# A two-layer streaming encoder in fp32: layer B's input projection computed from seven block products in place of eight

## The chip, the cores and the metric

One core of a Trainium2 chip runs the whole program. The metric is the device time of one execution in microseconds (us), the median of several runs. About 0.2% (4.5 us) is what a measurement of this kernel can tell from no change.

## The reference, cut to what matters

Two gated attention layers run over 2048 prompt frames and 64 sample frames (together 2112 tokens, width 1024). Each layer normalizes its input, projects it with one combined matrix, does banded attention, and projects back:

```python
def project(x, norm_g, w_in, q_g, k_g, n_heads, n_kv):
    h = rms_norm(x, norm_g)
    p = h @ w_in
    q, k, v, gate = jnp.split(p, [wq, wq + wkv, wq + 2 * wkv], axis=-1)
    q = rms_norm(q.reshape(*lead, n_heads, HEAD_DIM), q_g)
    k = rms_norm(k.reshape(*lead, n_kv, HEAD_DIM), k_g)
    return q, k, v, gate
# per layer: y = x + (attention(q, k, v) * silu(gate)) @ w_out
```

Layer A (first) has 16 heads on 2 key heads; layer B has 16 heads of 64 with their own keys. For layer B `w_in` is 1024 x 4096. For one pair of heads the columns of q, k, v and gate are 4 x 128 = 512.

## The kernel before, in words

Everything is computed in fp32 by splitting each operand into a high part and a low part (`h`, `l`, type fp32r, one pass of TensorE each) and adding three products: xh·wh, xh·wl, xl·wh.

**Layer B's projection.** The tokens are cut into eight units of 256 (two tiles of 128 tokens) and one sample unit of 64. The work runs over eight head pairs (`hp`, 0 to 7) and, inside a pair, over the nine units in the order 0 to 6, sample, 7. `project_b` (L513) computes one tile: eight blocks of 128 input features, three matmuls each of 512 columns (L527, L528, L529) into one PSUM bank (`pj`, two buffers). The stationary operand is a 128x128 block of x, the moving one a 128x512 block of the weights. `evacuate` (L622; the ACTIVATE at L635) copies the 512 columns to SBUF on ScalarE (ACT) with the tokens' RMS scale: 384 columns (q, k, v) and 128 (gate).

**Operands.** `load_b` (L542) gives a unit its four operands A11, A12, A21, A22: Aij is tile i (of two) and half j of the input features. In pair 0 they are loaded raw from `x1`, split by ACT (L553) and GpSimd (POOL, L554) into an `xx` buffer (seven of them, XN) and stored to `xo` in DRAM (512 KB each). From pair 1 on they are loaded from `xo` (L549). A unit's loads are issued when the unit before it starts.

**Weights.** `load_weights` (L282) prepares a pair's weights: eight raw loads of 256 KB, each scaled by the norm gain and split by ACT (L315) and VectorE (DVE, L318) into `wh` and `wl` (fifteen buffers each, WN). The first five are queued three units ahead, the rest one unit ahead.

**The order of the work.** TensorE (PE) follows the order in which the program is written: `Filler` (L761) hands out projection work in steps of three matmuls, and the attention pipeline (L1357) calls for a share of it between its own steps. Attention works two units behind the projection: per tile and head `scores` (L1244), then `values` (L1304, transposes and one copy at L1321: ACT for the unit's first tile, DVE for its second), then `outputs` (L1324). Side work (weights, splits, norms) goes into a background queue that is emptied in shares at these points. The other engines and the one DMA queue (SP) are ordered by the framework's scheduler at compile time. After layer B the output projection follows (L1441 to L1443).

Of the kernel before, what the change touches and what calls it, by code (L numbers as in the profile page):

```python
# [33 lines left out]
XB = 3  # L34
XR = 5
XN = 7
EARLY = 3
MORE = 4.7
WN = 15
# [14 lines left out]
def hybrid_encoder_kernel(  # L54
# [171 lines left out]
    og = [dr.tile([P, KC, TOK], F32, tag=n, name=n) for n in ("oga", "ogb")]  # L226
    x1 = dr.tile([P, KC, TOK], F32, tag="x1", name="x1")
    xs = dr.tile([P, 2 * KC * TOK], F32, tag="xsa", name="xsa")
    xo = dr.tile([P, 4 * NU + 1, 8 * P], F32, tag="xo", name="xo")

    class Item:
        pass
# [300 lines left out]
        res.append(ps)  # L533
        return cost

    SLOT = {n: i for i, n in enumerate(("A11", "A12", "A21", "A22"))}

    def operand(xx):
        v = xx[:, : 8 * P].rearrange("p (e k s) -> p e k s", e=2, k=4)
        return v[:, 0], v[:, 1]  # L540

    def load_b(unit, hp):  # L542
        u, T, tiles = unit
        x = Item()
        x.op, x.items = {}, []

        def cached(n, i):
            xx = t("xx", [P, 4 * OT], XN, F32R)
            held["last"] = load(xx[:, : 8 * P].bitcast(F32), xo[:, i]).ins  # L549
            return xx  # L550

        def split(xx, xh, xl, rv, i):
            nc.scalar.copy(xh, rv)  # L553
            nc.gpsimd.tensor_tensor(xl, rv, xh.bitcast(F32), op=ALU.subtract)  # L554
            store(xo[:, i], xx[:, : 8 * P].bitcast(F32))

        if T == TS:
            if hp:
                x.joint = cached("J", 4 * NU)[:, : 8 * P].rearrange("p (k s) -> p k s", k=8)
                return x  # L560
            raw = t("xraw", [P, 2 * OT], XR)[:, :512].rearrange("p (k s) -> p k s", k=8)
            held["last"] = load(raw, x1[:, :, SEQ:TOK]).ins

            def fn():
                xx = t("xx", [P, 4 * OT], XN, F32R)
                x.joint = v = xx[:, : 8 * P].rearrange("p (k s) -> p k s", k=8)
                split(xx, v[:, :, :TS], v[:, :, TS:], raw, 4 * NU)

            x.items.append(bg.put(0.52, fn))
            return x  # L570

        names = ("A11", "A12", "A21", "A22")
        raw = {}

        def raws():
            for e in range(2):
                for i in range(2):
                    r = t("xraw", [P, 2 * OT], XR)[:, :512].rearrange("p (k s) -> p k s", k=4)
                    held["last"] = load(r, x1[:, 4 * i : 4 * i + 4, u * UT + e * P : u * UT + e * P + P]).ins
                    raw["A%d%d" % (e + 1, i + 1)] = r  # L580

        def part(n, src):
            def fn():
                xx = t("xx", [P, 4 * OT], XN, F32R)
                xh, xl = operand(xx)
                split(xx, xh, xl, raw[src], 4 * u + SLOT[n])
                x.op[n] = xh, xl
            return fn

        if hp == 0:  # L590
            raws()
            x.items = [bg.put(0.52, part(n, n)) for n in names]
# [541 lines left out]
    def layer_b():  # L1134
# [4 lines left out]
        def add_unit(hp, unit):  # L1139
# [12 lines left out]

            def weights(*m):
                if hp not in st.emit:
                    (st.w[hp],), _, st.emit[hp] = load_weights(1, (w_in_b[hp], 512))
                st.emit[hp](*m)

            def take_qk(e, pr):
# [35 lines left out]
                    it.ready = e == len(tiles) - 1  # L1194
                    yield c

            filler.total += 8 * (6 if T == UT else 2) * 512 / 2400
            it.mark = filler.total
            filler.add(prefetch, weights if u == 0 else None, gen)

        for hp in range(8):
            for unit in order:
# [154 lines left out]
        def pipeline():  # L1357
# [231 lines left out]
```

## Time and profile before

| | |
|---|---|
| time, median of 3 runs | 2264.24 us (2262.56 to 2265.06) |
| time of the profiled execution | 2262.1 us |
| its span, first to last instruction | 2260.3 us |
| PE, DVE, ACT, POOL busy | 99%, 63%, 58%, 34% of the span |
| layer B's projection, eight pairs | 857.9 to 2047.9 us of the span |
| granted TensorE clock, mean | 0.997 |

A busy PE is counted from the start of a matmul to the modelled end of its drain, and successive matmuls overlap. So what one matmul costs in a stream is the distance between two starts, not its duration. Start times are in the timeline view.

### The profile page before, as it was taken

The numbers are of one execution on the slowest core, as the hardware profiler recorded it, in microseconds if no ns is written. First come the engines' busy times: TensorE is split into PE (matmuls) and PEld (weight loads), VectorE is DVE, ScalarE is ACT, GpSimd is POOL, SyncE is SP. The second block draws the span as 40 slices with busy tenths as digits, with TensorE's granted clock in tenths as the row PEclk, the third lists the DMA queues.
The fourth block names the chain that finished last, engine by engine and source line by source line (L and its number), as shares of the span: only waits on it lengthen the run. The fifth ranks groups of instructions, "written<-read, shape, count | busy, mean of one in ns | idle before, by whom it ended". The sixth has DMA issues, their size and how long they took to land. (4 is left out here: it accounts for less than half of the span.)

```text
span 2260.3 us, 41004 instructions
## 1 busy us (share of the span) xinstructions
PE 2231.6 (99%) x13981; PEld 1908.7 (84%) x13981; DVE 1423.0 (63%) x4168; ACT 1312.7 (58%) x3341; POOL 778.4 (34%) x1153
## 2 busy tenths in 40 slices
PE   8999999999999999999999999999999999999999
PEld 7887888888889998878888888888888888888999
DVE  7779988888785545675655655656556556565211
ACT  7888877777774335664555655545556555454321
POOL 5654533333254445431222222222222212223442
PEclk9999999999999999999999999999999999999999
DMA  8846446754446767554554544544545445443664
GB/s 281 298 144 214 165 139 184 224 179 146 158 121 193 215 188 268 186 182 142 150 148 138 158 139 142 151 145 142 148 140 160 138 137 154 139 125 113 201 182 135
DMA packets 236800, 379.26 MB, mean 168 GB/s; under 512 B 24288, under 2 KB 167024, under 8 KB 236560
## 3 DMA queue, kind: packets, MB, share of 16 engines
q1 hardware_dynamic: 236592, 376.65, 54.4%
q8 instruction: 110, 1.80, 0.3%
q14 instruction: 98, 0.80, 0.1%
HBM read 296.13 MB, written 82.08 MB: 167 GB/s over the span
## 5 line engine op out<-in xcount | busy, mean ns | idle before, releaser
L527 PE MATMUL pj<-wh,xx 128*128 128x512 f32 x1024 | 426.8, 417 | 0.0
L529 PE MATMUL pj<-wh,xx 128*128 128x512 f32 x1024 | 403.6, 394 | 0.0
L528 PE MATMUL pj<-wl,xx 128*128 128x512 f32 x1024 | 403.3, 394 | 0.0
L1285 ACT ACTIVATE p<-p,nm 128x640 f32<-128x640 f32 (+5 forms) x272 | 204.4, 751 | 236.9 <-DVE nm L1281 234.1
L1281 DVE CUSTOM_DVE_ANT_0 p<-sb,BT 128x640 f32<-128x640 f32 (+5 forms) x272 | 196.5, 722 | 173.3 <-PE sb L1275 169.5
L1441 PE MATMUL pj<-xx,wh 128*128 128x264 f32 x1024 | 295.0, 288 | 4.9 <-DVE res L1446 4.8
L389 POOL TENSOR_TENSOR xx<-xraw,xx 128x528 fp32r<-128x528 f32 (+1 forms) x168 | 225.1, 1362 | 202.9 <-ACT xx L388 197.4
L1442 PE MATMUL pj<-xx,wh 128*128 128x264 f32 x1024 | 292.1, 285 | 0.0
L1443 PE MATMUL pj<-xx,wl 128*128 128x264 f32 x1024 | 290.8, 284 | 0.0
L654 POOL TENSOR_TENSOR f<-f,mhalf 128x4 f32<-128x4 f32 (+1 forms) x136 | 137.4, 1011 | 428.9 <-DVE f L653 420.6
L613 PE MATMUL pj<-wh,xx 128*128 128x512 f32 (+1 forms) x624 | 245.9, 394 | 1.3 <-ACT pb L635 1.0
L614 PE MATMUL pj<-wl,xx 128*128 128x512 f32 (+1 forms) x624 | 233.0, 373 | 1.8 <-DVE wl L318 1.8
L615 PE MATMUL pj<-wh,xx 128*128 128x512 f32 (+1 forms) x624 | 234.1, 375 | 0.0
L527 PEld LDWEIGHTS pj<-wh,xx 128*128 128x128 f32 x1024 | 193.0, 188 | 44.9 <-issue 20.1
L529 PEld LDWEIGHTS pj<-wh,xx 128*128 128x128 f32 x1024 | 192.7, 188 | 44.8
L528 PEld LDWEIGHTS pj<-wl,xx 128*128 128x128 f32 x1024 | 193.7, 189 | 23.2
L1441 PEld LDWEIGHTS pj<-xx,wh 128*128 128x128 f32 x1024 | 193.6, 189 | 7.8 <-DVE res L1446 6.0
L635 ACT ACTIVATE pa<-pj,rms 128x384 f32<-128x384 f32 (+1 forms) x219 | 118.1, 539 | 136.7 <-PE pj L529 125.8
L1442 PEld LDWEIGHTS pj<-xx,wh 128*128 128x128 f32 x1024 | 193.3, 189 | 0.2
L1443 PEld LDWEIGHTS pj<-xx,wl 128*128 128x128 f32 x1024 | 193.5, 189 | 0.0
L388 ACT CAST xx<-xraw 128x528 fp32r<-128x528 f32 (+1 forms) x168 | 103.0, 628 | 133.0 <-PE pj L1443 112.9
L1040 ACT ACTIVATE p<-p,nm 128x257 f32<-128x257 f32 (+2 forms) x272 | 134.5, 497 | 73.5 <-DVE nm L1034 61.3
(228 smaller groups left out, 5222.1 us busy)
## 6 DMA issues: line engine op xcount, KB each, us to landing
xx<-xo SPq DMA_DIRECT2D x231, 512.0 KB, 3.6
xx<-xsa SPq DMA_DIRECT2D x88, 512.0 KB, 4.6
xraw<-oga SPq DMA_DIRECT2D x64, 264.0 KB, 3.5
xo<-xx SPq DMA_DIRECT2D x33, 512.0 KB, 4.4
xraw<-ogb SPq DMA_DIRECT2D x64, 264.0 KB, 3.4
xsa<-xx SPq DMA_DIRECT2D x32, 512.0 KB, 4.2
wraw<-in_w_in_b_dram SPq DMA_DIRECT2D x64, 256.0 KB, 3.1
xraw<-in_x_dram SPq DMA_DIRECT2D x40, 256.0 KB, 4.6
```

What stands on the lines that cost most here:

```text
L389: nc.gpsimd.tensor_tensor(xl, rv, xh.bitcast(F32), op=ALU.subtract)
L527: nc.tensor.matmul(ps, xh, wh, start=k == 0, stop=False)
L528: nc.tensor.matmul(ps, xh, wl, start=False, stop=False)
L529: nc.tensor.matmul(ps, xl, wh, start=False, stop=k == KC - 1)
L613: nc.tensor.matmul(ps[:n, :C], xh, wh, start=k == 0, stop=False)
L614: nc.tensor.matmul(ps[:n, :C], xh, wl, start=False, stop=False)
L615: nc.tensor.matmul(ps[:n, :C], xl, wh, start=False, stop=k == KC - 1)
L1281: mi = nc.vector.tensor_tensor_reduce(out=p[:n, :nk], in0=S[:n, o : o + nk], in1=bias[:n, b0 : b0 + nk], op0=ALU.add, op1=ALU.min, scale=1 ...
L1285: ex = nc.scalar.activation(p[:n, :nk], p[:n, :nk], AF.Exp, scale=-1.0, bias=nmh, accum_out=it.sm[:n, 2 * i + h : 2 * i + h + 1],)
L1441: nc.tensor.matmul(ps[:, :OT], wh, oh, start=k == 0, stop=False)
L1442: nc.tensor.matmul(ps[:, :OT], wh, ol, start=False, stop=False)
L1443: nc.tensor.matmul(ps[:, :OT], wl, oh, start=False, stop=k == KC - 1)
```

## The change

For pairs 2 to 7 and the eight prompt units, the 256 x 1024 by 1024 x 512 product is cut into 2 x 2 blocks (tokens, input features, output columns: q and k in the left half, v and gate in the right) and computed by Strassen's algorithm in Winograd's form, from seven block products (P1 to P7), each of four feature blocks, three matmuls and 256 columns, in place of eight. It needs four sums of x blocks (S1 to S4) and four of weight blocks (T1 to T4). Pairs 0 and 1 stay as they are, but make S1 to S4 on the side and store them in `xo`; units 6 and 7 do it in pair 0, units 0 to 5 in pair 1, which load the raw blocks again for it. From pair 2 on a unit loads seven operands. The sample unit is computed from the same weight pieces without sums. In these pairs the second tile's copies in `values` move from DVE to ACT.

```diff
+PLAIN = 2
+S_FIRST = (6, 7)
-    xo = dr.tile([P, 4 * NU + 1, 8 * P], F32, tag="xo", name="xo")
+    xo = dr.tile([P, 8 * NU + 1, 8 * P], F32, tag="xo", name="xo")
+    PIECE = dict(P1="11", P6="T2", P2="21", P7="T3", P5="T1", P4="T4", P3="22")
+    OPERAND = dict(P1="A11", P6="S2", P2="A12", P7="S3", P5="S1", P4="A22", P3="S4")
+    def block_weights(src):
+        def fetch():
+            order_ = [(b, a) for b in ("11", "12", "22", "21") for a in range(2)]
+            for x, (b, a) in enumerate(order_):
+                r = t("wraw", [P, 512], WB) if x < WB else t("xraw", [P, 2 * OT], XR)
...
+        def piece(n, a, b, scaled):
+            def fn():
+                q = w[n][a]
+                q.h = wh = t("wh", [P, 1, 512], WN, F32R)[:, 0].rearrange("p (k c) -> p k c", k=2)
+                q.l = wl = t("wl", [P, 1, 512], WN, F32R)[:, 0].rearrange("p (k c) -> p k c", k=2)
+                rv = raw[b, a]
+                if not scaled:
+                    nc.scalar.copy(wh, rv)
+                    nc.vector.tensor_tensor(wl, rv, wh.bitcast(F32), op=ALU.subtract)
+                    return
+                for j in range(2):
+                    s = g(int(b[0]), a, j)
+                    nc.scalar.activation(wh[:, j], rv[:, j], AF.Identity, scale=s)
+                    nc.vector.scalar_tensor_tensor(
+                        wl[:, j], rv[:, j], s, wh[:, j].bitcast(F32), op0=ALU.mult, op1=ALU.subtract
+                    )
+            return 0.8, fn, w[n][a]
+        def mix(dst, src_, other, a, op):
+            def fn():
+                for j in range(2):
+                    nc.vector.scalar_tensor_tensor(
+                        raw[dst, a][:, j], raw[src_, a][:, j], g(int(src_[0]), a, j), raw[other, a][:, j],
+                        op0=ALU.mult, op1=op,
+                    )
+            return 0.6, fn, None
...
+        two = range(2)
+        todo += [piece("11", a, "11", True) for a in two]
+        todo += [f(a) for a in two for f in (scaled_12, lambda a: mix("12", "22", "12", a, ALU.subtract))]
+        todo += [mix("11", "11", "12", a, ALU.add) for a in two]
+        todo += [piece("T2", a, "11", False) for a in two]
+        todo += [piece("21", a, "21", True) for a in two]
+        todo += [mix("21", "21", "11", a, ALU.subtract) for a in two]
+        todo += [piece("T3", a, "12", False) for a in two]
+        todo += [mix("11", "22", "11", a, ALU.subtract) for a in two]
+        todo += [piece("T1", a, "11", False) for a in two]
+        todo += [piece("T4", a, "21", False) for a in two]
+        todo += [piece("22", a, "22", True) for a in two]
...
+    def product(ps, xc, parts, p, start):
+        xh, xl = xc.op[OPERAND[p]]
+        for k in range(4):
+            wh, wl = parts(PIECE[p], k)
+            nc.tensor.matmul(ps[:, :256], xh[:, k], wh, start=start and k == 0, stop=False, skip_group_check=not start)
+            nc.tensor.matmul(ps[:, :256], xh[:, k], wl, start=False, stop=False, skip_group_check=not start)
+            nc.tensor.matmul(ps[:, :256], xl[:, k], wh, start=False, stop=k == 3, skip_group_check=not start)
+            if k < 3:
+                yield 3 * 256 / 2400
...
+        def sums():
+            for dst, a, b, op in (
+                ("A22", "A21", "A22", ALU.add), ("A21", "A11", "A21", ALU.subtract),
+                ("A11", "A22", "A11", ALU.subtract), ("A12", "A12", "A11", ALU.subtract),
+            ):
+                def fn(dst=dst, a=a, b=b, op=op):
+                    nc.vector.tensor_tensor(raw[dst], raw[a], raw[b], op=op)
+                bg.put(0.6, fn)
+            for n, src in (("S1", "A22"), ("S3", "A21"), ("S2", "A11"), ("S4", "A12")):
+                bg.put(0.52, part(n, src, False))
...
+            if u in S_FIRST and PLAIN < 8:
+                sums()
+        elif hp < PLAIN:
+            for n in names:
+                x.op[n] = operand(cached(n, 8 * u + SLOT[n]))
+            if u not in S_FIRST and PLAIN < 8:
+                raws()
+                sums()
         else:
-            for n in names:
-                x.op[n] = operand(cached(n, 4 * u + SLOT[n]))
+            for n in OPERAND.values():
+                x.op[n] = operand(cached(n, 8 * u + SLOT[n]))
...
+            def gen_blocks():
+                def scaled(ps, r):
+                    a = t("ev", [P, 256], 4)
+                    nc.scalar.activation(a, ps[:, :256], AF.Identity, scale=r)
+                    return a
+                A, B = psum("pj", 512, 2), psum("pj", 512, 2)
+                yield from product(A, xc, parts, "P1", True)
+                p1, s1 = scaled(A, r0), scaled(A, r1)
+                yield cost
+                yield from product(B, xc, parts, "P6", True)
+                p6 = scaled(B, r0)
+                nc.gpsimd.tensor_tensor(p6, p1, p6, op=ALU.add)
+                yield cost
+                yield from product(A, xc, parts, "P2", False)
+                pr = t("pa", [P, 384], 4)
+                nc.scalar.activation(pr[:, :256], A[:, :256], AF.Identity, scale=r0)
+                take_qk(0, pr)
+                yield cost
+                yield from product(B, xc, parts, "P7", False)
+                p7 = scaled(B, r1)
+                nc.gpsimd.tensor_tensor(p7, s1, p7, op=ALU.add)
+                yield cost
+                A = psum("pj", 512, 2)
+                yield from product(A, xc, parts, "P5", True)
+                vg = t("pb", [P, 256], 6)
+                nc.vector.scalar_tensor_tensor(vg, A[:, :256], r1, p7, op0=ALU.mult, op1=ALU.add)
...
+                yield from product(B, xc, parts, "P4", False)
+                pr = t("pa", [P, 384], 4)
+                nc.vector.scalar_tensor_tensor(pr[:, :256], B[:, :256], r1, s1, op0=ALU.mult, op1=ALU.add)
...
+                yield from product(A, xc, parts, "P3", False)
+                vg = t("pb", [P, 256], 6)
+                nc.vector.scalar_tensor_tensor(vg, A[:, :256], r0, p6, op0=ALU.mult, op1=ALU.add)
...
-            copy = (nc.scalar.copy, nc.vector.tensor_copy)[i]
+            copy = nc.scalar.copy if i == 0 or it.hp >= PLAIN else nc.vector.tensor_copy
...
+                    if its[x + 2].hp >= PLAIN and len(heads) == 4:
+                        end = c0 + 0.875 * PACE_B * len(heads)
```

## Rows read from the trace of the kernel before

**Rows 1.** The page, busy time of each engine.

```profile
PE 2231.6 (99%) x13981; PEld 1908.7 (84%) x13981; DVE 1423.0 (63%) x4168; ACT 1312.7 (58%) x3341; POOL 778.4 (34%) x1153
```

**Rows 2.** Windows, pair 3: stretch, length, PE PEld DVE ACT POOL busy, clock, DMA, GB/s.

```profile
1294.70:1445.30 150.60, 150.50 (x909) 122.95 (x907) 88.38 (x237) 82.65 (x210) 33.88 (x64) 1.00 0.49 146
```

**Rows 3.** Timeline of PE in pair 4: start, duration; 256 columns, then 512.

```profile
1509.27 0.28 PE L1274 MATMUL sb<-KA,q 128*128 128x256 f32 x1
...
1509.74 0.40 PE L527 MATMUL pj<-wh,xx 128*128 128x512 f32 x1
...
1510.90 0.40 PE L529 MATMUL pj<-wh,xx 128*128 128x512 f32 x1
```

**Rows 4.** Timeline of PE in layer A: 256 columns, transposes, 512 columns.

```profile
65.81 0.28 PE L615 MATMUL pj<-wh,xx 128*128 128x256 f32 x1
...
66.88 0.28 PE L615 MATMUL pj<-wh,xx 128*128 128x256 f32 x1
67.00 1.03 PE L743 MATMUL sa<-ident,p 128*128 128x128 f32 x8
67.79 0.48 PE L613 MATMUL pj<-wh,xx 128*128 128x512 f32 x1
68.10 0.39 PE L614 MATMUL pj<-wl,xx 128*128 128x512 f32 x1
```

**Rows 5.** Timeline of PE in the output projection: 264 columns.

```profile
2159.79 0.29 PE L1442 MATMUL pj<-xx,wh 128*128 128x264 f32 x1
...
2165.99 0.28 PE L1442 MATMUL pj<-xx,wh 128*128 128x264 f32 x1
```

**Rows 6.** Lines of pair 3, ACT: count, busy us, mean ns, idle before.

```profile
L1285 ACT ACTIVATE p<-p,nm 128x640 f32<-128x640 f32 x24 | 19.9, 829 | 22.1 <-DVE nm L1281 22.0
L635 ACT ACTIVATE pa<-pj,rms 128x384 f32<-128x384 f32 x17 | 9.9, 580 | 17.3 <-PE pj L529 16.1 <-PE pj L523 0.9
...
L635 ACT ACTIVATE pb<-pj,rms 128x128 f32<-128x128 f32 x17 | 6.1, 361 | 0.0
...
L1321 ACT COPY pl<-sb 128x640 f32<-128x640 f32 x6 | 4.1, 691 | 4.3 <-PE sb L743 4.2
```

**Rows 7.** Lines of pair 3, DVE.

```profile
L1231 DVE SCALAR_TENSOR_TENSOR q<-tp,qsc,q 64x256 fp32r<-64x256 f32 x16 | 7.7, 483 | 1.9 <-ACT KB L1227 1.6
...
L318 DVE SCALAR_TENSOR_TENSOR wl<-wraw,gain,wh 128x512 fp32r<-128x512 f32 x8 | 5.9, 750 | 0.1
...
L1321 DVE COPY pl<-sb 128x640 f32<-128x640 f32 x6 | 4.9, 821 | 1.6 <-PE sb L743 1.4
```

**Rows 8.** Lines of the whole run, shapes kept apart.

```profile
L1130 POOL TENSOR_TENSOR o<-gt,o 128x256 f32<-128x256 f32 x64 | 53.4, 834 | 146.9 <-ACT p L1040 103.7 <-DVE o L1129 9.9 <-ACT wh L310 9.2
...
L554 POOL TENSOR_TENSOR xx<-xraw,xx 128x512 fp32r<-128x512 f32 x33 | 43.2, 1331 | 17.7 <-ACT xx L553 17.7
...
L635 ACT ACTIVATE pa<-pj,rms 128x256 f32<-128x256 f32 x83 | 39.2, 472 | 3.0 <-PE pj L615 1.4
...
L680 DVE SCALAR_TENSOR_TENSOR pb<-sq,pb 128x256 f32<-128x256 f32 x64 | 26.7, 418 | 1.2 <-ACT sq L679 0.6
```

**Rows 9.** Windows, pair 3's first unit and its last (columns as in rows 2).

```profile
1294.70:1313.90 19.20, 19.20 (x123) 15.80 (x122) 10.61 (x32) 10.71 (x28) 5.17 (x13) 1.00 0.44 127
...
1426.00:1445.30 19.30, 19.30 (x121) 15.87 (x119) 13.83 (x33) 11.19 (x26) 5.94 (x11) 1.00 0.54 167
```

**Rows 10.** Windows, two changes of weights in layer A.

```profile
190.00:220.00 30.00, 26.83 (x141) 21.16 (x140) 27.99 (x90) 26.20 (x68) 11.37 (x17) 1.00 0.59 189
...
490.00:520.00 30.00, 29.41 (x161) 23.65 (x160) 28.32 (x97) 24.27 (x68) 9.92 (x16) 1.00 0.65 208
```

**Rows 11.** Waits of pair 3: total us, times, longest.

```profile
ACT pa L635 <- PE pj L529: 16.1, 6, 3.7
```

**Rows 12.** The page, DMA issues: count, KB, median us to landing.

```profile
xx<-xo SPq DMA_DIRECT2D x231, 512.0 KB, 3.6
```

**Rows 13.** Windows, pair 0's first unit (columns as in rows 2).

```profile
857.90:871.60 13.70, 13.70 (x60) 11.25 (x59) 4.31 (x10) 4.98 (x13) 7.64 (x7) 0.88 1.02 352
```

More of the change, by code (lines that the diff above doesn't have):

```diff
@@ L558, in load_b @@
             if hp:
-                x.joint = cached("J", 4 * NU)[:, : 8 * P].rearrange("p (k s) -> p k s", k=8)
+                x.joint = cached("J", 8 * NU)[:, : 8 * P].rearrange("p (k s) -> p k s", k=8)
                 return x
@@ L580, in raws, with part @@
                     raw["A%d%d" % (e + 1, i + 1)] = r
-        def part(n, src):
+        def part(n, src, keep):
             def fn():
@@ L585, in fn @@
                 xh, xl = operand(xx)
-                split(xx, xh, xl, raw[src], 4 * u + SLOT[n])
-                x.op[n] = xh, xl
-            return fn
+                split(xx, xh, xl, raw[src], 8 * u + SLOT[n])
+                if keep:
+                    x.op[n] = xh, xl
+            return fn
+        def sums():
[8 more added lines that the diff above has]
+                bg.put(0.52, part(n, src, False))
         if hp == 0:
             raws()
-            x.items = [bg.put(0.52, part(n, n)) for n in names]
-        else:
-            for n in names:
-                x.op[n] = operand(cached(n, 4 * u + SLOT[n]))
+            x.items = [bg.put(0.52, part(n, n, True)) for n in names]
+            if u in S_FIRST and PLAIN < 8:
[6 more added lines that the diff above has]
+                sums()
+        else:
+            for n in OPERAND.values():
+                x.op[n] = operand(cached(n, 8 * u + SLOT[n]))
         return x
@@ L1154, in weights @@
                 if hp not in st.emit:
-                    (st.w[hp],), _, st.emit[hp] = load_weights(1, (w_in_b[hp], 512))
+                    if hp < PLAIN:
+                        (st.w[hp],), _, st.emit[hp] = load_weights(1, (w_in_b[hp], 512))
+                    else:
+                        st.w[hp], st.emit[hp] = block_weights(w_in_b[hp])
                 st.emit[hp](*m)
@@ L1195, in gen, with gen_sample, run @@
                     yield c
-            filler.total += 8 * (6 if T == UT else 2) * 512 / 2400
+            def gen_sample():
+                xc = st.x.pop((hp, u))
+                it.prs, it.gate, it.todo = {}, {}, []
+                parts = st.w[hp]
+                cost = 2 * 256 / 2400
+                n = TS
+                sc = rr[1][:, NT : NT + 1]
+                def run(ps, name, k0, start):
+                    for k in range(4):
+                        wh, wl = parts(name, k)
+                        xk = xc.joint[:, k0 + k]
+                        if start and k == 0:
+                            nc.tensor.matmul(ps[:, :256], xk, wh, start=True, stop=False)
+                        nc.tensor.matmul(
+                            ps[:n, :256], xk[:, :n], wl, start=False, stop=False, skip_group_check=not start
+                        )
+                        if not (start and k == 0):
+                            nc.tensor.matmul(
+                                ps[:, :256], xk, wh, start=False, stop=k == 3, skip_group_check=not start
+                            )
+                        if k < 3:
+                            yield cost
+                A, B = psum("pj", 512, 2), psum("pj", 512, 2)
+                yield from run(A, "11", 0, True)
+                p1 = t("ev", [P, 256], 4)
+                nc.scalar.activation(p1, A[:, :256], AF.Identity, scale=sc)
+                nc.vector.tensor_tensor(p1[:n], p1[:n], p1[n:], op=ALU.add)
+                yield cost
+                yield from run(B, "T1", 0, True)
+                yield cost
+                yield from run(A, "21", 4, False)
+                pr = t("pa", [P, 384], 4)
+                nc.scalar.activation(pr[:, :256], A[:, :256], AF.Identity, scale=sc)
+                nc.vector.scalar_tensor_tensor(
+                    pr[:n, :256], A[:n, :256], sc[:n], pr[n:, :256], op0=ALU.mult, op1=ALU.add
+                )
+                take_qk(0, pr)
+                yield cost
+                yield from run(B, "22", 4, False)
+                vg = t("pb", [P, 256], 6)
+                nc.scalar.activation(vg, B[:, :256], AF.Identity, scale=sc)
+                nc.vector.scalar_tensor_tensor(
+                    vg[:n], B[:n, :256], sc[:n], vg[n:], op0=ALU.mult, op1=ALU.add
+                )
+                nc.vector.tensor_tensor(vg[:n], vg[:n], p1[:n], op=ALU.add)
+                take_vg(0, vg[:, 0:P], vg[:, P : 2 * P])
+                keep_kv(0, vg[:, 0:P])
+                it.ready = True
+                yield cost
@@ L1198, in add_unit @@
+            if T < UT:
+                it.cost = 8 * 2 * 512 / 2400
+            else:
+                it.cost = (8 * 6 * 512 if hp < PLAIN else 7 * 12 * 256) / 2400
+            filler.total += it.cost
             it.mark = filler.total
-            filler.add(prefetch, weights if u == 0 else None, gen)
+            filler.add(prefetch, weights if u == 0 else None, gen if hp < PLAIN else gen_blocks if T == UT else gen_sample)
         for hp in range(8):
```

56 lines of the change are left out of this document (54 added, 2 removed).

## The prediction

> **What bounds the kernel now.** I read the page first: PE is busy for 99% of the span, DVE for 63%, ACT for 58% [rows 1]. Then the windows of one head pair of layer B: PE 150.50 of 150.60 us, DVE 88.4, ACT 82.7, POOL 33.9, the DMA engines 0.49 [rows 2]. So in the part that changes, PE alone sets the pace. A busy PE can hide pauses, so the third view is the timeline: from 1509.74 to 1510.90 lie five steps of 512-column matmuls, 0.232 us each [rows 3], and nothing stands between them. What ends last is PE's own work. Fewer column passes shorten the kernel as long as the other engines hand PE its inputs and empty its PSUM banks in time.
>
> **A. PE.** A prompt unit takes 2 tiles x 8 blocks x 3 = 48 matmuls of 512 columns now, and 7 x 4 x 3 = 84 of 256 afterwards. The price of one at 256 columns is in layer A, where the key projection runs in this form with a new stationary block for each: nine steps from 65.81 to 66.88, 0.119 us [rows 4]. Unit before: 48 x 0.232 = 11.14 us; after: 84 x 0.119 = 10.00; gain 1.15. Over 8 units x 6 pairs = 48 units that is 55 us. Bounds: the scores' four steps of 0.117 [rows 3] give 9.87 and 61 us; 51 steps of 264 columns in 6.20 us, 0.122 each [rows 5], give 10.2 and 43 us. I take 55, as rows 4 have the same operands. The sample unit issues the same columns as before (32 x 256 for 16 x 512): nothing.
>
> The number of weight loads goes up by 84/48, and that speaks against the change. Eight transposes of 128 columns take from 67.00 to 67.79, 0.099 us each, though they stream half of 256 columns: there the load sets the pace [rows 4]. At 0.119 the stream just covers it. The change pays up to 11.14/84 = 0.133 us per matmul. The Trainium skill, page "TensorE: Matmul & The Clock Gate", section "Back-to-back issue gap", gives for streams of load and matmul about 81 ns at 128 columns and 131 ns at 512; an estimate between them is 98 ns at 256, by which a unit would go from 6.3 to 8.2 us and the kernel lose some 93 us. This trace does not agree: 232 ns at 512 and 119 at 256, nearly in proportion to columns.
>
> **B. Emptying PSUM.** Now two copies of a tile, 0.580 + 0.361 us on ACT [rows 6], have a whole tile (24 x 0.232 = 5.6 us) until the bank is needed. Afterwards each product is emptied while only one other product runs: 12 x 0.119 = 1.43 us, plus the attention steps between. ACT gets five copies of 256 columns per unit, 0.472 each [rows 8], DVE three operations from PSUM at 0.483 [rows 7], POOL two additions at 0.834 [rows 8]. The tightest is P1, two copies in a row. Lower bound: nothing (a gain is excluded, since the copies only add waits). Upper: an exponential of 0.829 [rows 6] just ahead, then 2 x 0.472, is 1.77; over 1.43 by 0.34 us, x 48 = 16 us. I take 4 us, near the lower end: in this pair ACT six times stood idle until the matmul it evacuates had ended [rows 11], so it comes at once when free.
>
> Average load afterwards, per pair of 141 us: ACT 82.7, plus 8 x (5 x 0.472 - 2 x 0.941) = 4, plus 16 copies moved from DVE at 0.691 [rows 6] = 11, plus about 6 for weights, 104 (73%). DVE 88.4 - 16 x 0.821 + 24 x 0.483 + 12 for weights (below) = 99 (70%). POOL 34 + 16 x 0.834 = 47. Neither is a bound on average: in layer A PE keeps 29.41 of 30 us with DVE at 28.32 [rows 10].
>
> **C. The change of weights, once per pair.** DVE's weight work is 8 x 0.750 = 6.0 us now [rows 7]. Afterwards: 12 scaled halves at 0.418 [rows 8] = 5.0, eight unscaled pieces at 0.750 = 6.0, sixteen half sums at 0.418 = 6.7; together 17.7, so 12 more. It cannot be spread: 14 pieces live in 15 buffers, so only one can be made before the last unit has used its first product, and each later one follows a release. About 14 us fall into that last unit, where DVE has 13.83 us now, 2.25 of it weights [rows 9] (an estimate: three of the eight). That makes 11.6 + 14 = 25.6 in a unit of 19.3 - 1.15 = 18.1: 7.5 too much. Behind the pieces on DVE stand the score minima and the three PSUM reads, and PE waits for those. The next unit has 19.2 - 1.15 - 10.6 = 7.4 us to spare [rows 9]. Bounds per change: 0 if all of the surplus slips there behind the pipeline's slack, 7.5 if none does. I take 3: in layer A's changes of weights PE lacks 0.6 us with DVE at 28.3 of 30 and 3.2 with DVE at 28.0 and ACT at 26.2 [rows 10]; here both are as full, so the second. Six changes: 18 us (0 to 45).
>
> **D. The first two pairs and the DMA queue.** Per unit the sums cost DVE 4 x 0.75, POOL 4 x 1.331 [rows 8], ACT four casts, and SP four loads of 256 KB (in pair 1, again) and four stores of 512 KB. Pair 1 moves about 146 GB/s x 17.3 us = 2.5 MB a unit, as pair 3 [rows 2]; with 3.1 MB more that is 326 GB/s for six units. Pair 0's first unit ran 352 GB/s at a DMA share of 1.02 with PE 13.70 of 13.70 us [rows 13]. Bounds: 0, and half a landing of 3.6 us [rows 12] late in each of six units, 11. I take 2. From pair 2 on seven loads in place of four make 2.5 + 1.6 MB in 16 us, 255 GB/s; free. Seven buffers for seven operands let a load start when the same product of the unit before is done, six products ahead of its use, some 14 us against 3.6. On SP the loads wait for those releases in order; what queues behind them (weight loads, bias tiles, attention stores) has a unit's slack. If that cover went, a late operand would cost PE directly.
>
> **Sum.** -55 + 4 + 18 + 2 = -31 us, against the profiled execution's own 2262.1 (span 2260.3): 2231. The median of the runs is 2.1 us above that execution; I carry it along: 2233.
>
> **Rivals.**
> *Clean.* Slack absorbs C, and D is nothing: -55 + 2 = -53, 2211. For it: layer A's second change of weights lost 0.6 us only [rows 10], and attention runs two units behind. Against: 25.6 us of work in 18.1.
> *DVE bound at the change of weights.* The whole 7.5 us each time: -55 + 45 + 4 + 2 = -4, 2260. For it: work released piece by piece comes ahead of later attention work. Against: the unit behind it has room.
> *Slower: late PSUM banks.* If ACT or DVE let each of the seven products wait, the gain is gone at (55 - 18 - 2)/336 = 0.10 us per product; at 0.2 us it is 67 us, so -55 + 18 + 2 + 67 = +32, 2296. For it: a fourth of the cover of now, ACT at 73%, in strict order. Against: rows 11, and the attention steps that lengthen the cover.
> *No gain on PE.* The 256-column matmul costs 0.133 because loads no longer hide: the terms B to D alone, +24, 2288. Rows 4 speak against it. By the figures of the Trainium skill given above it would be some 2357.
>
> **Chances.** Forecast 0.45 (2216 to 2250), clean 0.25, DVE bound 0.14, late banks 0.12, no gain on PE 0.04. The range 2204 to 2260 holds the first three with their bounds and leaves out the last two. About 0.2% (4.5 us) is what a measurement can tell from no change: 2260 to 2269 is the same. Faster: 0.45 + 0.25 + 0.10 of the third case = 0.80; same 0.04 + 0.02 = 0.06; slower 0.14.
>
> **What would show it.** Right: the new matmuls 0.118 to 0.120 apart; pairs 2 to 7 some 145 us long in place of 150.6, the missing part of the gain in the last unit and the next one, with DVE near full there; pair 1 hardly longer. Wrong: steps of 0.13 or more; waits of PE for `pj` copies spread over all units; PE waiting for `xx` loads in pair 1; or DVE with room left at the change of weights, which would make the gain 50 us and more.

## The result, and the profile after

| | before | after |
|---|---|---|
| median | 2264.27 us (2262.56 to 2265.06) | 2294.93 us (2293.31 to 2295.61) |
| span of the profiled execution | 2260.3 us | 2293.8 us |
| granted TensorE clock, mean | 0.997 | 0.989 |
| pairs 0 to 7, first projection matmul to the next pair's (pair 7: to its last matmul's end) | 138.6, 147.6, 150.6, 150.6, 150.4, 150.4, 150.5, 151.3 | 141.4, 161.6, 152.2, 155.1, 153.4, 152.6, 154.9, 148.3 |

The change makes the kernel slower: ratio 1.0135, interval 1.0118 to 1.0153. The forecast was 2233. So the time went up by 31 us where it should have come down by 31. Below, the page of the changed kernel; PE had been busy for 99% [rows 1].

```profile
span 2293.8 us, 46036 instructions
PE 2206.8 (96%) x15805; PEld 1993.3 (87%) x15805; DVE 1547.5 (67%) x4428; ACT 1440.4 (63%) x3619; POOL 908.5 (40%) x1281
```

The cheaper matmuls are there. In the timeline of PE (start, duration) the steps of 256 columns lie 0.12 us apart, as in layer A [rows 4]:

```profile
1485.82 0.28 PE L627 MATMUL pj<-wh,xx 128*128 128x256 f32 x1
1485.94 0.28 PE L628 MATMUL pj<-wl,xx 128*128 128x256 f32 x1
1486.06 0.28 PE L629 MATMUL pj<-wh,xx 128*128 128x256 f32 x1
1486.18 0.28 PE L627 MATMUL pj<-wh,xx 128*128 128x256 f32 x1
```

What is new is PE waiting. Its largest waits from 1144 to 2060 us, that is nearly to the end of layer B's projection (total us, times, longest); before the change, none was listed from 1144 to 2040 us:

```profile
PE pj L627 <- DVE pb L1399: 19.9, 6, 3.7
PE pj L627 <- ACT ev L1376: 10.3, 10, 2.2
PE pj L627 <- DVE pb L1358: 4.6, 5, 1.0
PE pj L1328 <- DVE pb L1411: 4.3, 6, 0.8
```

L1399 is DVE's read of product P5 from its PSUM bank; the next product that needs the bank is P3. It is late by 3.7 us in the last unit of each of pairs 2 to 6, and once by 1.5 us in pair 2's third unit. The units of pair 4 took 18.9, 17.7, 16.1, 14.6, 16.5, 18.2, 20.2, 6.5 and **24.7** us; of a pair before, 19.1, 18.0, 17.3, 15.3, 17.6, 18.8, 19.3, 5.8 and 19.3. So the first six units are shorter, unit 6 and the sample unit are 0.9 and 0.7 us longer, and the last one, in which most of the next pair's weights are made, is 5.4 us longer. The windows of the changed kernel: pair 1, pair 4, and the last unit of pair 4 in fives (busy time and instructions of PE, PEld, DVE, ACT, POOL; granted clock; DMA share; GB/s):

```profile
1002.00:1163.60 161.60, 151.15 (x871) 122.02 (x870) 117.70 (x276) 95.22 (x236) 67.25 (x85) 0.98 0.78 260
...
1471.00:1624.40 153.40, 145.17 (x1211) 135.96 (x1210) 104.05 (x274) 100.94 (x252) 48.56 (x81) 0.99 0.73 224
...
1600.00:1605.00 5.00, 4.06 (x33) 3.85 (x32) 4.94 (x15) 4.36 (x11) 2.01 (x3) 1.00 0.73 211
1605.00:1610.00 5.00, 5.00 (x47) 4.01 (x46) 4.68 (x11) 4.49 (x11) 2.27 (x3) 1.00 0.50 149
1610.00:1615.00 5.00, 4.99 (x42) 4.78 (x41) 4.87 (x13) 4.94 (x11) 0.44 (x1) 1.00 0.63 169
1615.00:1620.00 5.00, 2.17 (x18) 1.80 (x16) 4.88 (x11) 1.49 (x4) 0.30 (x1) 1.00 0.65 199
1620.00:1625.00 5.00, 4.14 (x21) 4.14 (x22) 4.81 (x12) 4.96 (x12) 3.32 (x4) 0.66 0.91 289
```

DVE is nearly full for 25 us (24.2 busy), PE idles in the fourth row, and after the wait the granted clock is down: 0.66 in the fifth. It stands at half, 1.2 GHz in place of 2.4, from 1621.2 to 1624.6 us:

```profile
1621.20:1624.60 3.40, 3.40 (x17) 3.40 (x16) 3.21 (x9) 3.40 (x9) 2.98 (x4) 0.50 0.87 294
```

The timeline of PE shows wait and clock together, steps of 0.21 us in place of 0.12:

```profile
1616.89 0.28 PE L629 MATMUL pj<-wh,xx 128*128 128x256 f32 x1
1620.86 0.39 PE L627 MATMUL pj<-wh,xx 128*128 128x256 f32 x1 [3.69 <-DVE pb L1399]
...
1622.70 0.41 PE L628 MATMUL pj<-wl,xx 128*128 128x256 f32 x1
1622.91 0.41 PE L629 MATMUL pj<-wh,xx 128*128 128x256 f32 x1
```

P5's last matmul had started at 1614.74 us. DVE's timeline shows what stands ahead of the read of its bank (L1399, the last row): low parts of the new weights (L567), half sums for them (L580), and a score minimum (L1505):

```profile
1617.12 0.69 DVE L567 TENSOR_TENSOR wl<-wraw,wh 128x512 fp32r<-128x512 f32 x1
1617.73 0.68 DVE L567 TENSOR_TENSOR wl<-xraw,wh 128x512 fp32r<-128x512 f32 x1
1618.33 0.48 DVE L580 SCALAR_TENSOR_TENSOR wraw<-xraw,gain,wraw 128x256 f32<-128x256 f32 x1
1618.73 0.42 DVE L767 TENSOR_REDUCE f<-sq 128x4 f32<-128x256 f32 x1
1619.17 0.82 DVE L1505 CUSTOM_DVE_ANT_0 p<-sb,BT 128x640 f32<-128x640 f32 x1
1619.92 0.08 DVE L1505 DVE_READ_ACCUMULATOR2_ANT nm<- 128x1 f32 x1
1619.92 0.48 DVE L580 SCALAR_TENSOR_TENSOR wraw<-xraw,gain,wraw 128x256 f32<-128x256 f32 x1
1620.32 0.48 DVE L1399 SCALAR_TENSOR_TENSOR pb<-pj,rms,ev 128x256 f32<-128x256 f32 x1
```

### The profile page after: what moved, and what is told of

It reads as the page before. It is cut to its first block, busy times and chain, and to the rows that moved or that the text cites. A ratio compares the mean times of both kernels' runs of the same rounds, so it can differ in the third digit from the quotient of the medians.

```text
span 2293.8 us, 46036 instructions
## 1 busy us (share of the span) xinstructions
PE 2206.8 (96%) x15805; PEld 1993.3 (87%) x15805; DVE 1547.5 (67%) x4428; ACT 1440.4 (63%) x3619; POOL 908.5 (40%) x1281
## 5 line engine op out<-in xcount | busy, mean ns | idle before, releaser
L627 PE MATMUL pj<-wh,xx 128*128 128x256 f32 x1344 | 404.9, 301 | 39.8 <-DVE pb L1399 20.3
L629 PE MATMUL pj<-wh,xx 128*128 128x256 f32 x1344 | 382.5, 285 | 0.0
L628 PE MATMUL pj<-wl,xx 128*128 128x256 f32 x1344 | 381.9, 284 | 0.0
L627 PEld LDWEIGHTS pj<-wh,xx 128*128 128x128 f32 x1344 | 257.5, 192 | 63.5 <-DVE pb L1399 21.8
L1505 DVE CUSTOM_DVE_ANT_0 p<-sb,BT 128x640 f32<-128x640 f32 (+5 forms) x272 | 196.6, 723 | 103.2 <-PE sb L1499 99.9
L628 PEld LDWEIGHTS pj<-wl,xx 128*128 128x128 f32 x1344 | 258.2, 192 | 0.0
L629 PEld LDWEIGHTS pj<-wh,xx 128*128 128x128 f32 x1344 | 257.7, 192 | 0.0
L769 POOL TENSOR_TENSOR f<-f,mhalf 128x4 f32<-128x4 f32 (+1 forms) x136 | 144.0, 1059 | 154.3 <-DVE f L768 146.6
L858 PE MATMUL sb<-ident,p 128*128 128x128 f32 x1168 | 174.6, 275 | 9.9 <-DVE ph L1545 9.8
L1672 DVE TENSOR_TENSOR res<-pj,res 128x264 f32<-128x264 f32 x128 | 55.0, 430 | 190.8 <-PE pj L1669 186.8
```

What stands on the lines that cost most here:

```text
L627: nc.tensor.matmul(ps[:, :256], xh[:, k], wh, start=start and k == 0, stop=False, skip_group_check=not start)
L628: nc.tensor.matmul(ps[:, :256], xh[:, k], wl, start=False, stop=False, skip_group_check=not start)
L629: nc.tensor.matmul(ps[:, :256], xl[:, k], wh, start=False, stop=k == 3, skip_group_check=not start)
L1505: mi = nc.vector.tensor_tensor_reduce(out=p[:n, :nk], in0=S[:n, o : o + nk], in1=bias[:n, b0 : b0 + nk], op0=ALU.add, op1=ALU.min, scale=1 ...
```

## The experiments

My theory: the block products pay as forecast; the five changes of weights behind them (at the ends of pairs 2 to 6) and the sums in pair 1 cost more. "Pairs" below are lengths as in the table. A run without an interval is one execution, and its pairs are those of that execution. How far such lengths scatter: in e1 and e4, whose edits do not touch pair 1, it took 162.8 and 163.1 us, where the changed kernel's took 161.6.

### The change of weights

**e1_weights_once**: pairs 3 to 7 use pair 2's pieces again, so five changes of weights are gone (the output is that of other weights).

```diff
-                    else:
+                    elif hp == PLAIN:
                         st.w[hp], st.emit[hp] = block_weights(w_in_b[hp])
+                    else:
+                        st.w[hp], st.emit[hp] = st.w[PLAIN], lambda *m: None
```

> The changed kernel, but pairs 3 to 7 use the weight pieces of pair 2 again, so that five of the six changes of weights cost nothing (the projection of pairs 3 to 7 is computed with pair 2's weights). Theory 'change of weights': the units around it (6, sample, 7), 52 us together in pair 4, go to about 42, and pairs 3 to 6 to some 143 us; the kernel to about 2245 us. Rival 'late banks': products wait for PSUM all over the units, the pairs stay near 153 us and the time near 2290.

2247.49 us, against 2263.0 before on the same chip. Pairs 3 to 6 take 143.4, 143.3, 143.4, 143.3 (154.0 on average in the changed kernel): a change of weights costs 10.6 us. Without it the last unit takes 17.7 us. The window of its pair 4, then its largest waits from 1163 us on:

```profile
1454.10:1597.40 143.30, 142.25 (x1212) 134.24 (x1211) 88.01 (x238) 90.14 (x228) 44.85 (x79) 1.00 0.73 226
```

```profile
PE pj L1330 <- DVE pb L1413: 4.3, 6, 0.8
PE pj L627 <- ACT ev L1378: 2.0, 7, 0.5
PE pj L627 <- ACT pa L1391: 1.7, 1, 1.7
```

DVE's weight work is 104.05 - 88.01 = 16 us per pair. In pair 4 the listed waits of PE are 8.0 us in the changed kernel and 1.0 here. Of the other 3 us between 153.4 and 143.3, the stretch at half the clock costs about 1.6; the rest is in pauses that the list leaves out.

**h4_no_mix**: the sixteen half sums of a change are left out, all else stays.

```diff
         def mix(dst, src_, other, a, op):
             def fn():
-                for j in range(2):
-                    nc.vector.scalar_tensor_tensor(...)
+                pass
```

> The sixteen half sums of the weights (DVE, about 0.42 to 0.6 us each) are left out at each of the six changes of weights; everything else is the changed kernel. Theory 'DVE's weight work holds the last unit': some 8 us less on DVE, the last unit of pairs 2 to 6 at 20 to 21 us in place of 24.7, each of these pairs some 5 us shorter, the kernel at 2265 to 2270. Rival 'the pieces themselves (buffers, order) hold it': the last unit stays above 23.5 us and the kernel above 2285.

2264.04 us; last units 19.0 to 19.1, pairs 3 to 6 148.8 on average. Its pair 4, and its two largest waits in that pair:

```profile
1452.90:1602.80 149.90, 145.14 (x1210) 136.03 (x1210) 97.96 (x259) 100.68 (x252) 47.21 (x79) 0.99 0.74 230
```

```profile
PE pj L623 <- ACT ev L1372: 3.5, 3, 2.1
PE pj L1324 <- DVE pb L1407: 0.8, 1, 0.8
```

Six microseconds of DVE less (97.96 for 104.05) and the wait for P5's bank is gone: 5.2 of the 10.6 us. The rest stays with ACT, whose reads of the products are late (3.5 us), above all in unit 6. ACT's timeline in the changed kernel's pair 4 shows why: its work for the next pair's weights (a high part at L571, scaled raw blocks at L589) stands ahead of its read of P6 (L1376), and PE waits 2.1 us for that read.

```profile
1577.90 0.89 ACT L571 ACTIVATE wh<-wraw,gain 128x256 fp32r<-128x256 f32 x2
1578.70 0.89 ACT L589 ACTIVATE wraw<-wraw,gain 128x256 f32<-128x256 f32 x2
1580.07 0.91 ACT L589 ACTIVATE xraw<-xraw,gain 128x256 f32<-128x256 f32 x2
1580.88 0.46 ACT L1376 ACTIVATE ev<-pj,rms 128x256 f32<-128x256 f32 x1
```

**e4_copies_dve**: the second tile's copies go back from ACT to DVE.

```diff
-            copy = nc.scalar.copy if i == 0 or it.hp >= PLAIN else nc.vector.tensor_copy
+            copy = (nc.scalar.copy, nc.vector.tensor_copy)[i]
```

> The changed kernel with the second tile's copies of the attention weights back on DVE. Theory 'change of weights' with DVE as the full engine: two copies of 0.82 us more in the full unit and the one before, so some 2 us more at each of six changes, about 2307 us. Rival: ACT, strictly in order and 73% loaded, is the late one, and the time falls to about 2285 us.

2300.84 us, 5.9 more, which is half of what was expected. But 3.6 of it lie in pairs 0 and 1, whose copies the edit leaves alone, and pairs 3 to 6 take 153.7 on average (154.0 in the changed kernel). The load moves between two late engines. The last unit takes 25.0 to 25.5 in pairs 3 to 6, and PE's waits for P5's bank grow from 19.9 to 23.7 us; unit 6 falls to 18.4 (20.2 to 21.7), and the waits for ACT at L1376, 10.3 us in the changed kernel, are gone (6.6 us for its other read, L1389, come in). So ACT is the late one in unit 6, DVE in the last.

**f1_low_pool**: the low parts of the four sums' pieces (unscaled) on POOL.

```diff
-                    nc.vector.tensor_tensor(wl, rv, wh.bitcast(F32), op=ALU.subtract)
+                    nc.gpsimd.tensor_tensor(wl, rv, wh.bitcast(F32), op=ALU.subtract)
                     return
```

> The changed kernel, with the low parts of the eight unscaled weight pieces of a pair (T1 to T4) computed on POOL instead of DVE: about 6 us per pair leave DVE, nearly all of it from the full unit. Theory 'change of weights, DVE full': a change costs about 5 us less, six of them 25 to 30 us, and the time is 2265 to 2270 us. Rival: ACT, as full as DVE in that unit, holds the time near 2290.

A miss: 2313.41 us, last units 25.7 to 26.6, and PE still waits 3.9 us for P5's bank in pair 4. What DVE was spared came back as longer instructions. The timelines of DVE and of POOL there (start, duration; a half sum L580 takes 0.48 and a cast L1463 0.29 otherwise):

```profile
1613.60 2.46 DVE L580 SCALAR_TENSOR_TENSOR wraw<-wraw,gain,xraw 128x256 f32<-128x256 f32 x1
...
1624.02 1.28 DVE L1463 CAST q<-q 64x256 fp32r<-64x256 f32 x1
```

```profile
1613.37 1.17 POOL L769 TENSOR_TENSOR f<-f,mhalf 64x4 f32<-64x4 f32 x1
1614.52 1.26 POOL L567 TENSOR_TENSOR wl<-wraw,wh 128x512 fp32r<-128x512 f32 x1
...
1623.67 1.48 POOL L567 TENSOR_TENSOR wl<-xraw,wh 128x512 fp32r<-128x512 f32 x1
```

DVE's half sum begins inside one instruction of POOL and ends just behind the next one (1616.06 after 1615.78); the cast begins inside one and ends just behind it (1625.30 after 1625.15).

**f8_mix_pool**: raw blocks scaled once and the half sums made 512 wide, both on POOL; low parts stay on DVE.

```diff
+        def scale(b, a):
+                nc.gpsimd.tensor_tensor(raw[b, a], raw[b, a], s, op=ALU.mult)
         def mix(dst, src_, other, a, op):
+                nc.gpsimd.tensor_tensor(raw[dst, a], raw[src_, a], raw[other, a], op=op)
```

> The changed kernel, with the weight work of a pair shared out anew: the raw blocks are scaled on POOL three units ahead, the sums of blocks made on POOL, each piece copied on ACT and its low part made on DVE. DVE's weight work falls from some 20 us a pair to 10, ACT's from 12 to 8.5, POOL gets about 20. Theory 'change of weights, DVE full': units 6, sample and 7 fall from 52 to 45 us or less, five changes save 30 us, and the time is about 2262 us. Rival: work on POOL only makes another queue late, as with the low parts on POOL, and the time is over 2290 us.

2271.19 us (before: 2263.44); pairs 3 to 6 147.7 to 150.1, last units 21.0 to 21.7. Of the 31 us lost 24 are back, but PE still waits up to 2.3 us for P5's bank, 14.7 us in all, and DVE's low parts of 128x512 take 0.82 to 1.05 us on average in place of 0.70 to 0.81. Its waits from 1160 us on begin with

```profile
PE pj L618 <- DVE pb L1390: 14.7, 8, 2.3
```

**f7_prescaled_all**: the half sums on DVE, the scaling and the sums' low parts on POOL, and all operand sums in pair 0.

```diff
+        todo += [piece("T2", a, "11", pool) for a in two]
-S_FIRST = (6, 7)
+S_FIRST = (0, 1, 2, 3, 4, 5, 6, 7)
```

> Sums of all units in pair 0, and the weights prepared otherwise: the raw blocks are scaled on POOL three units ahead, then every piece is a copy on ACT, the low parts of T1 to T4 on POOL, the others and the sums of blocks on DVE over 512 columns. DVE's weight work in the full unit falls from some 16 us to about 8. Theory 'change of weights': the units 6, sample and 7 go from 52 to about 43 us, pairs 2 to 6 to some 145 us, the time to about 2240 us, below both kernels. Rival: POOL, with 19 us of weight work more per pair, becomes the late one, and the time stays above 2264 us.

A miss: 2295.15 us, ratio 1.0139 (1.0117 to 1.0161). Last units 22.1 to 24.9, the first units of pairs 2 to 6 21.2 to 24.6 (18 to 19 in the changed kernel); pair 0 155.2.

### The operand sums

**e2_sums_alone**: all pairs plain, the sums still made.

```diff
-PLAIN = 2
+PLAIN = 8
-            if u in S_FIRST and PLAIN < 8:
+            if u in S_FIRST:
```

> All eight pairs projected as before the change, but S1 to S4 are still made and stored in pairs 0 and 1 (nobody reads them). Theory 'sums': pairs 0 and 1 take about 17 us more than before, the time is about 2281 us, and pairs 2 to 7 stay at 150.5 us. Rival: the sums are hidden when nothing else of the change is there, and the time is 2264.

2283.28 us: pairs 0 and 1 take 142.3 and 162.5, the rest 150.3 to 151.2. Alone, the sums cost some 19 us (304.8 - 286.2).

**e3_no_sums**: no sums; plain blocks are multiplied in their place (so they are not the products of the sums, but equal in number and size).

```diff
-                x.op[n] = operand(cached(n, 8 * u + SLOT[n]))
+                x.op[n] = operand(cached(n, 8 * u + SLOT[n] % 4))
```

> The changed kernel without S1 to S4: they are neither made nor stored, and from pair 2 on the plain blocks of the same unit are loaded in their place (the seven products use wrong operands). Theory 'sums': pair 1 goes back from 161.6 to about 148 us, and the time to about 2277 us. Rival: pair 1 is long for another reason, the time stays at 2295.

2279.92 us; pairs 139.5, 151.7, 149.6, 155.2, 152.5, 155.7, 152.3, 147.8. So pairs 0 and 1 lose 12 us less and the later ones stay as they were: two separate costs. The 5.0 us that pairs 0 and 1 lose even here hold the first change of weights, which falls at the end of pair 1 (its last unit takes 21.7 for 18.8 before).

**f3_first_all**: all sums in pair 0 (the second part of f7's diff).

> The changed kernel, with S1 to S4 of all eight units made in pair 0, where the raw blocks are in SBUF already, and nothing of it in pair 1. Theory 'DVE stands behind the second load of the raw blocks in a full DMA queue': pair 1 falls from 161.6 to about 149 us, pair 0 grows by 2 to 4 us, the time is about 2285 us. Rival: the work itself (POOL 5.3 us and 2 MB of stores a unit) is the cost and only moves to pair 0: 2295 us.

2294.31 us: pair 0 154.7, pair 1 151.4. The cost moves with the sums.

**f9_deferred**: a unit's sums in pair 1 are traced one unit after their raw loads.

```diff
                 raws()
-                sums()
+                deferred.append(sums)
```

> The changed kernel, with the sums of a unit in pair 1 traced one unit after their raw blocks are loaded, so that DVE and ACT never stand behind that load; the same instructions and bytes. Theory 'DVE stands behind the load': pair 1 falls from 161.6 to about 152 us and the time to about 2286 us. Rival: the full DMA queue itself (0.91 busy) holds PE, and pair 1 stays above 158 us.

2294.38 us, pair 1 163.0. DVE's waits for raw loads fall from 8.3 to 2.1 us, and ACT waits 11.7 us for stores to give `xx` buffers back: the wait moved.

**g1_no_store**, **h1_no_pool**, **h2_sums_only**, **h3_splits_only**: parts of the sums left out (e3's edit stands in each).

```diff
-                split(xx, xh, xl, raw[src], 8 * u + SLOT[n])
+                nc.scalar.copy(xh, raw[src])
+                nc.gpsimd.tensor_tensor(xl, raw[src], xh.bitcast(F32), op=ALU.subtract)
```

g1 is this, without the store; h1 drops the second added line too, h2 ACT's line as well; h3 is g1 without DVE's `tensor_tensor` in `sums`.

> The four operand sums of each unit are computed as in the changed kernel, but their stores of 512 KB each are left out, and from the third pair on the plain blocks' copies are loaded in their place (same number and size of loads), so the output is not that of the reference. Theory 'store traffic': pair 1 (161.6 us with the stores, DMA share 0.91) is long because stores of 2 MB a unit fill the DMA queue and hold back the raw loads; without them pair 1 comes down to 150 or 152 us and the kernel to about 2284. Rival 'work of the sums': DVE, ACT and POOL and the raw loads set it; pair 1 stays at 158 to 162 us, the kernel at 2291 to 2295. Pairs 2 to 7 as in the changed kernel, 152 to 155 us.

> As the run without stores (2296.0, pair 1 162.9 us), and POOL's subtraction for the four sums of a unit is left out too; loads of raw blocks, DVE's sums and ACT's casts stay. Theory 'POOL slows DVE': with 24 subtractions of 1.4 us less on POOL in pair 1, DVE's casts are back at 280 to 300 ns and the additions of 128x512 at 0.68, pair 1 comes to 153 to 156 us and the kernel to about 2288. Rival 'DVE waits in order behind raw loads': nothing changes, pair 1 stays at 160 to 163 us, the kernel at 2294 to 2297.

> The same with ACT's casts left out as well: of the operand sums only the raw loads and DVE's four additions per unit stay (24 in pair 1, 17 us of DVE). Theory 'POOL slows DVE': pair 1 at 151 to 154 us, as in the run without POOL or a little less. Rival 'DVE waits in order behind raw loads': pair 1 at 158 to 162 us, since both the loads and the additions are there.

> The other half: raw loads, ACT's casts and POOL's subtractions stay, DVE's additions and the stores are left out. Theory 'POOL slows DVE': DVE's casts at 400 ns and more, pair 1 at 154 to 157 us. Rival 'DVE waits in order behind raw loads': no DVE instruction waits for a raw load any more, pair 1 at 150 to 152 us, the kernel at about 2284.

| | sums' parts that stay, beside the raw loads | pair 1 | time |
|---|---|---|---|
| changed kernel | DVE, ACT, POOL, stores | 161.6 | 2294.93 |
| g1 | DVE, ACT, POOL | 162.9 | 2296.0 |
| h1 | DVE, ACT | 160.3 | 2290.61 |
| h3 | ACT, POOL | 157.8 | 2285.06 |
| h2 | DVE | 152.0 | 2285.41 |

Without stores the DMA share from 1002 to 1064 us falls from 0.91 to 0.62 and pair 1 does not move: the stores are out. POOL's part does slow DVE. DVE's lines from 1002 to 1163 us, in the changed kernel and then in h1 (count, busy us, mean ns):

```profile
L692 DVE TENSOR_TENSOR xraw<-xraw,xraw 128x512 f32<-128x512 f32 x24 | 18.6, 777 | 8.7 <-DMA xraw<-x 8.3
L786 DVE TENSOR_TENSOR pa<-pa,f 128x256 f32<-128x256 f32 (+1 forms) x16 | 8.9, 556 | 5.5 <-POOL f L769 5.5
L1455 DVE SCALAR_TENSOR_TENSOR q<-tp,qsc,q 64x256 fp32r<-64x256 f32 (+1 forms) x18 | 8.3, 461 | 0.2
L1463 DVE CAST q<-q 64x256 fp32r<-64x256 f32 (+1 forms) x18 | 8.1, 448 | 0.5
```

```profile
L789 DVE TENSOR_TENSOR pa<-pa,f 128x256 f32<-128x256 f32 (+1 forms) x16 | 6.8, 422 | 6.8 <-POOL f L772 6.6
L1458 DVE SCALAR_TENSOR_TENSOR q<-tp,qsc,q 64x256 fp32r<-64x256 f32 (+1 forms) x18 | 8.3, 461 | 0.3
L1466 DVE CAST q<-q 64x256 fp32r<-64x256 f32 (+1 forms) x18 | 5.0, 278 | 1.0 <-ACT q L1453 0.5
```

But with that gone pair 1 still takes 160.3 us, so neither theory as written holds. ACT's casts with their `xx` buffers are worth most (160.3 to 152.0). DVE's additions and the raw loads cost nothing by themselves: h2 has both, and its pair 1 is as long as e3's without any of it (151.7). In h1 the raw loads wait 10.5 us on SP's queue (1000 to 1046 us) for those casts to free raw buffers, which led to the next run.

**i1_more_raw**: seven raw buffers in place of five, six `xx` in place of seven.

```diff
-XR = 5
-XN = 7
+XR = 7
+XN = 6
```

> The changed kernel with seven buffers for raw blocks in place of five and six for operands in place of seven; nothing is left out. Theory 'raw buffers': the next unit's raw loads no longer wait for the casts of the unit before, DVE's additions find their blocks there, pair 1 comes from 161.6 to 153 to 156 us and the kernel to about 2288 (if six operand buffers are enough for the block products; otherwise pairs 2 to 7 get longer). Rival 'work of DVE, ACT and POOL': pair 1 stays at 159 to 163 us.

2286.01 us, but pair 1 is 159.7: of the 9 us the theory earns 2, hardly more than the scatter. Pairs 3 to 6 stay at 154.2 on average, so raw buffers do not hold the change of weights either. DVE no longer waits for raw loads (0.2 us in place of 8.3), yet PE waits as before, for reads that stand behind work on DVE. Its two largest waits from 1000 to 1163 us:

```profile
PE sb L858 <- DVE ph L1545: 4.6, 2, 2.4
PE tp L858 <- DVE KB L1459: 3.2, 1, 3.2
```

### Both together

**f10_both** (f8 and f9), **g2_three_pairs** (f8, sums over pairs 1 and 2, block products from pair 3) and **i2_more_raw_mix_pool** (f8 and i1):

```diff
-PLAIN = 2
+PLAIN = 3
-            if u not in S_FIRST and PLAIN < 8:
+            if u not in S_FIRST and (u < 3) == (hp == 1):
```

> Both of these edits together. If both theories hold, pairs 2 to 6 come to some 147 us, pair 1 to 152, and the time to about 2253 us, below the kernel before the change (2264); if POOL is the new late queue, it stays above 2280 us.

> Sums of the weights on POOL (as in f8_mix_pool, 2271.2), and the operand sums of the units other than the last two spread over pairs 1 and 2, three units each, with the block products from pair 3 on. Theory 'the queue has to be full': with three units of sums in a pair instead of six, each of the two pairs loses 2 us or less against its plain 150.5, the sums cost about 7 us in all instead of 18, and with five pairs at some 148.5 us the kernel comes to 2262 to 2267. Rival 'each unit of sums costs its share': 2 us for each of the six units wherever it is put, 156 us in pairs 1 and 2, and with one pair's gain of 2 lost 2270 to 2276.

> The same buffers, together with the half sums of the weights on POOL (f8_mix_pool, 2271.2 us with pair 1 at 158.7). Theory 'raw buffers': pair 1 at 153 us, 2264 to 2267, level with the kernel before. Rival 'work': 2270 to 2273, as without the buffers.

f10: 2276.18 us, ratio 1.0063 (1.0047 to 1.0080). g2: 2277.95, 1.0060 (1.0043 to 1.0077). Its pairs are known only from its longest execution, 2288.04 us. There pair 1 with three units of sums takes 159.1, as f8's with six (158.7): its first three units are 11.5 us longer than before. Pair 2, with the other three and the first change of weights, takes 159.5, of which those three units are 4.2 and the last unit 4.8. Both expectations miss. i2: 2273.58, 1.0041 (1.0027 to 1.0055), with pair 1 at 157.2: its rival held. No variant that computes the reference's output beats the kernel before.

## Why the prediction was wrong

The account by pairs: e1's pairs 2 to 7 sum to 865.2 us against 903.8 before, so the products with what they wait for bring -38.6 (A and B: -51 forecast). The changed kernel's pairs 2 to 7 sum to 916.5, so five changes of weights cost 51.3 (C: 18 for six). Pairs 0 and 1 cost 303.0 - 286.2 = 16.8 (D: 2); some 12 of it are the sums by e3 (alone, in e2, they cost 19), and the rest holds the sixth change. Layer B starts 2.7 us later, and what follows it takes 1.2 more. In all 33.4, against 33.5 between the spans.

**A was right**: steps of 0.119 to 0.12 us as taken from rows 4, and loads that stay hidden. The rival without a gain on PE falls. By these steps a pair would gain 9.2 us; in e1 pair 4 gains 7.1 (143.3 for 150.4), and B has to answer for the difference.

**B was right in kind, small in size.** PE's waits in e1 sum to 9.0 us (4 forecast, 0 to 16). Nearly half is one place I costed at nothing, the sample unit: its second product waits 0.7 us for DVE's read of P3 (L1411; L1413 in e1), six times, and that unit takes 6.5 us in place of 5.8. Of the 12 us by which A and B fall short, the waits explain 5; the other 7 no row here assigns.

**C is the step that failed: "I take 3" per change, where the runs show 10.6.** The work itself was well sized: 16 us of weights on DVE per pair (17.7 forecast), DVE 104 us in all (99), ACT 101 (104), POOL 49 (47). Wrong was the slack. I let the surplus slip into the next unit, as attention two units behind allows, and chose the lower price by likeness to layer A [rows 10]. But DVE took its work in the order in which it was queued, and in the last unit the weight pieces stood ahead of the PSUM reads: P5's last matmul started at 1614.74, its bank was read at 1620.32. A bank that is read late has no unit of slack, only the one product between, as B itself had said (1.43 us). So the surplus came out at the banks: in pair 4 3.7 us at P5 and 0.9 behind the sample unit's read, which e1 lacks. My upper end, 7.5, is DVE's alone and lacked two parts: 2.6 us of waits for ACT's reads, most of them in unit 6, where I had counted ACT's weight work into an average and at nothing where it falls; and the granted clock, which is at half behind the long wait, some 1.6 us in pair 4. h4 shows the half sums alone to hold half of the 10.6.

**D was wrong in size and in mechanism.** I priced late landings in the DMA queue (0 to 11 us) and counted engine work as hidden. The queue did fill (0.91 of the share, operands landing after 7.1 us where 3.6 was typical [rows 12]), but g1 emptied it and gained nothing. Pair 1 is long in its first three units (20.3, 20.8 and 21.5 us for 15.3, 19.8 and 17.3 before). PE's longest wait there, 3.2 us, is for the copy in the last of these rows of DVE; ahead of it stand a wait for a raw load, an addition for the sums and a cast at several times its 0.29 us:

```profile
1040.87 0.69 DVE L692 TENSOR_TENSOR xraw<-xraw,xraw 128x512 f32<-128x512 f32 x1 [3.23 <-DMA xraw<-x]
...
1042.34 1.40 DVE L1463 CAST q<-q 64x256 fp32r<-64x256 f32 x1
...
1046.80 0.82 DVE L1545 COPY ph<-sb 128x640 f32<-128x640 f32 x1
```

That this order of work on DVE, ACT and POOL makes all of the cost is my reading. Taken away in part, it gives back little: h1 and i1 1 to 2 us, which is within the scatter, and h3 4. h2 gets all back but the 4 that e3 has as well. Which of ACT's time and the `xx` buffers that its casts hold makes the difference between h1 and h2 is not separated; buffers of their own for the sums were not tried.

**The slower rival** gave 2296 and was near in time by chance: its mechanism was a wait at each of the seven products in every unit. Late banks it is, some 40 us of PE's waits, but 35 of them are the first three of its rows above, which e1, without the changes, all but lacks. The "DVE bound" rival named the right place and priced it too low.

The Trainium skill, page "SBUF — State Buffer", section "SBUF: two separate sides", says that VectorE and GpSimd share a port pair: a VectorE instruction with two SBUF inputs, or in a two-port mode, and a GpSimd instruction that reads SBUF exclude each other on it, and whichever starts first holds it for its whole length while the other blocks. The rows of f1 agree as far as POOL's rough spans can show it: DVE's instructions end 0.15 to 0.28 us behind POOL's. By that rule every addition that this change puts on POOL can hold DVE up, and the prediction did not weigh it.

## What to carry to other kernels

Price new work on an engine that takes its work in order by what stands behind it with the least cover, in the stage where it falls, not by the engine's share over the pair. A PSUM bank with one product of cover cannot lend slack, however idle the next unit is. And a saving on the bounding engine has to be set against all work that prepares it: here 39 us won on PE were paid for with 16 us of DVE work, and ACT's beside it, at each change of weights, and with a set of sums that nothing hid.

## What the hardware showed beyond that

- Some instructions of DVE between SBUF and SBUF lengthen while POOL runs two-operand operations (a half sum of 0.48 us took 2.46). In pair 1, each shape by itself, the addition of 128x256 (`pa`) took 436 ns before, 566 in the changed kernel, 669 in g1, 724 in h3, and 422 in h1 and h2, where POOL's subtractions are left out; the cast of 64x256 took 289, 422, 483, 523 and again 289. The reduction of 128x256 (`f<-sq`) did not change (412 to 417), nor did the operation of 64x256 that reads PSUM (483 to 484).
- A wait of PE can cost more than its length: after 3.69 us of waiting the granted clock over the next five microseconds was 0.66 and steps of 256 columns took 0.21 us. Without the changes of weights (e1) the clock stays at 1.00 all through pair 4. It does not follow every wait. Behind the wait of 2.1 to 2.2 us in unit 6 the clock was 0.50 in pairs 3 and 6 (1426.6 to 1430.0 and 1887.4 to 1890.8 us), where that unit took 21.7 us, and 1.00 in pairs 4 and 5, where it took 20.2.
